# A two-layer encoder step: early convolution taps on ScalarE and GpSimd, later taps summed in PSUM, memory values and some keys as three split products, layer-norm sums added up before TensorE

## The chip, the cores and the metric

The kernel runs on one core of a Trainium2 chip. A core has a matrix engine (TensorE, PE in the profile), a vector engine (VectorE, DVE), a scalar engine (ScalarE, ACT), a general engine (GpSimd, POOL) and a queue that issues transfers (SyncE, SP). Each engine takes its own instructions strictly in order and waits on semaphores for the others. Data lies in SBUF, matrix products go to eight banks of PSUM (128 partitions by 512 words each). The metric is the device time of one launch in microseconds; lower is better. The trace comes from one profiled execution, whose span runs from the first to the last instruction.

## What is computed

One inference step of two layers for two groups that share all weights: 8 running streams of 16 tokens ("sample", 128 tokens) and one new stream of 256 tokens ("prompt"). So all work is on 384 tokens, in three token tiles of 128, with 1024 features.

```python
for i in range(DEPTH):                     # 2 layers
    x = x + 0.5 * rms_norm(swiglu(rms_norm(x)))
    if i % 2 == 0: y = conformer_conv_module(rms_norm(x), ...)
    else:          y = gated_deltanet(rms_norm(x), ...)
    x = x + rms_norm(y)
    x = x + rms_norm(memory_cross_attention(rms_norm(x), mem_k[i], mem_v[i]))
    x = x + 0.5 * rms_norm(swiglu(rms_norm(x)))

# conformer_conv_module
u = h @ w_in + b_in
val, gate = jnp.split(u, 2, axis=-1)
u = val * jax.nn.sigmoid(gate)
hist = jnp.concatenate([conv_buf, u], axis=1)      # 30 earlier rows, then this step's
c = causal_depthwise_conv(hist, dw) + dw_b         # 31 taps per feature
c = jax.nn.silu(layer_norm(c, ln_g, ln_b))
return c @ w_out + b_out, hist[:, -30:]
```

The memory keys and values of the prompt, `p_mem_k` and `p_mem_v`, are 256 memory tokens times one 1024 x 1024 matrix each per layer. They are outputs, and the cross-attention of the prompt reads them back. The sample's come from a cache.

## The kernel before

**Recording and ordering.** The program is first recorded as a list of operations (`Emitter`), and a list scheduler (`Scheduler`) then puts them in order on each engine, by the longest way to the end on costs written in the file. Once ordered, each engine's instructions stand fixed. What waits for nothing else goes where the scheduler sees an engine without other work.

**Weights.** A weight chunk is 128 x 1024 words (512 KB). `get` loads it into one of three raw buffers; ScalarE casts it to the reduced matmul type (the high part, `whi`, line 189) and VectorE subtracts the high part from the raw words (the low part, `wlo`, line 197). Both inputs of that subtraction lie in SBUF. Eight split chunks are held at a time. A product of a chunk and split activations is three matmuls: high times high, high times low, low times high (`gmm`, `dmm`, line 247).

**Memory keys and values.** There are 32 pieces of 128 output features: 8 for keys and 8 for values in each layer. `kv(n)` records the next n of them in plain float32: 16 matmuls of 128 columns each, which show as two records each in the trace. They need only the memory and a raw weight chunk, no splitting, and so can fill TensorE at any time. The table `KV` says how many each place offers: 3 at the start, 3 behind the first feed-forward layer, 20 in the convolution (`conv`), 3 ahead of its output projection (`co`), 1 and 2 behind the next two feed-forward layers.

**The convolution module.** `conv` runs over 8 feature tiles of 128. For each tile two projections (`cg`, `cv`, 24 matmuls of 384 columns each) give gate and value; `glu` makes the sigmoid on ScalarE and two products on VectorE, and copies the prompt's rows into overlapping windows (`h`). `taps` then handles the tiles in pairs. The first 15 taps (`TOLD`) reach only earlier tokens of a sample stream and were already summed for the sample part in `old_taps`, during the feed-forward layer. For the prompt, tap 0 is a `tensor_scalar` of 256 columns and taps 1 to 14 are multiply-adds of 240 down to 227 columns; taps 15 to 30 are 16 multiply-adds of 384 columns (both groups). All of them are on VectorE (lines 204 and 210) and add into `cO` in SBUF, with two tensor inputs in SBUF. Behind each tile one float32 matmul of 384 columns by a matrix of 1/1024 adds its features into the mean, 8 in all.

**Layer norm and output projection.** `ln(t)`, for each token tile: VectorE subtracts the mean, ScalarE squares, 8 float32 matmuls of 128 columns add up the squares, VectorE and GpSimd make the root, one matmul spreads it, VectorE multiplies, ScalarE applies SiLU (8 instructions) and casts, VectorE subtracts for the low part. The output projection (chunks `co`) can begin with the first cast, `hTh`. Nothing else of the program can run on TensorE between the last convolution projection and that point, apart from memory pieces, the layer norm's own matmuls and a bias row (`ones_r`).

Of the kernel before, what the change touches and what calls it, by code (L numbers as in the profile page):

```python
# [58 lines left out]
# constant matrices: causal blocks, block sums, decay masks, block-doubling masks  # L59
# [8 lines left out]
def chunk_names():  # L68
    names = [("mem", 0), ("mem", 1), ("bout",)]
    for l in range(2):  # L70
        for i in range(2):
            for f in range(FF):
                names += [("g", l, i, f), ("u", l, i, f), ("d", l, i, f)]
            names += [(n, l, i, j) for n in ("g4", "u4") for j in range(4)]
        names += [("q4", l, 0, j) for j in range(4)]
        for k in range(KT):
            names += [("wq", l, k), ("wo", l, k), ("wk", l, k // 2, k % 2), ("wv", l, k // 2, k % 2)]
# [16 lines left out]
class Emitter:  # L94
    """Records the program in issue order. Tasks beside the main stream are advanced by running
    clocks of the engines, so that their matmuls fall where their operands are ready."""
# [153 lines left out]
    def quad(self, mms):  # L250
        """Products into four groups of 32 rows, which the tensor engine works on at once."""
# [1538 lines left out]
```

## Time and profile before

| | |
|---|---|
| three runs | 1892.46, 1894.15, 1896.69 us; median 1894.15 us |
| profiled execution | span 1891.9 us |
| median less span | 2.25 us |
| records of TensorE / VectorE / ScalarE / GpSimd | 10863 / 1940 / 1589 / 407 |
| mean granted TensorE clock | 0.998 |
| transfers | 278.83 MB, 147 GB/s over the span |

How to read the views quoted below: a line of the timeline has the start in us from the span's start, the length in us, the engine, the line of the file, the operation, output and inputs (partitions x columns), the number of instructions merged in it, and in brackets how long the engine had stood idle and what released it. A group line has, behind the bar, the busy time in us and the mean ns of one instruction, then the idle time before them. A row of the windows view has the stretch, its length, and the busy time of TensorE, its weight loads, VectorE, ScalarE and GpSimd, the granted clock, the share of the transfer engines and GB/s. Instructions of one engine overlap a little, so the distance between starts is shorter than the mean length. A float32 matmul shows as two records.

### The profile page before, as it was taken

How to read it: one execution, taken by the hardware profiler on the slowest of the kernel's cores; microseconds unless marked ns; L12 is line 12 of the kernel's file. 1: busy time of each engine (PE TensorE's matmuls, PEld its weight loads, DVE VectorE, ACT ScalarE, POOL GpSimd, SP SyncE). 2: the span in 40 equal slices, each digit the busy share in tenths (PEclk: the TensorE clock that was granted, in tenths of full speed). 3: DMA queues.
4: the chain of work that ended last, by engine and by line, in shares of the span. 5: the costliest groups of instructions: out<-in, count | busy, mean ns of one | idle time of the engine just before them, and what ended most of it. 6: DMA issues, size and time to landing. Idle time of an engine off the chain costs nothing.

```text
span 1891.9 us, 27912 instructions
## 1 busy us (share of the span) xinstructions
PE 1870.6 (99%) x10863; PEld 1682.6 (89%) x10863; DVE 1025.5 (54%) x1940; ACT 794.5 (42%) x1589; POOL 168.8 (9%) x407
## 2 busy tenths in 40 slices
PE   8999999999999999999999999999999999999998
PEld 7999999999877899999899999989898767899997
DVE  6564436998653633334633344788886734533333
ACT  4333334312643533233433233787786533433332
POOL 1000002111100100000100000323321101000000
PEclk9999999999999999999999999999999999999999
DMA  8544434556685443434533343433324782444431
GB/s 300 179 136 125 134 112 121 128 147 216 219 312 210 156 129 128 134 123 130 163 122 117 120 134 101 128 97 99 123 90 124 236 311 101 134 134 134 122 123 45
DMA packets 88469, 278.83 MB, mean 147 GB/s; under 512 B 18001, under 2 KB 20561, under 8 KB 88337
## 3 DMA queue, kind: packets, MB, share of 16 engines
q1 hardware_dynamic: 86080, 271.42, 44.7%
q0 software_dynamic: 2256, 5.64, 0.9%
q8 instruction: 85, 1.39, 0.3%
q14 instruction: 48, 0.39, 0.1%
HBM read 265.09 MB, written 11.92 MB: 146 GB/s over the span
## 4 chain that ended last, share of the span: by engine, by line
PE 97%; ACT 1%; DMA 1%; DVE 0%; POOL 0%; issue 0%; SPq 0%; DVEq 0%; POOLq 0%; ACTq 0%
PE ps L247 91%; PE ps L266 3%; PE ps L259 2%; DMA raw<-in_w 0%; POOL stat L197 0%; ACT big L190 0%; DMA x<-in_x 0%; DVE big L210 0%; ACT whi L189 0%; SPq L270 0%; ACT big L189 0%; ACT hTl L190 0%; ACT L190 0%; DVE big L197 0%; DVE wlo L197 0%
## 5 line engine op out<-in xcount | busy, mean ns | idle before, releaser
L197 DVE TENSOR_TENSOR wlo<-raw,whi 128x1024 fp32r<-128x1024 f32 x361 | 438.1, 1221 | 570.7 <-ACT whi L189 542.7
L189 ACT CAST whi<-raw 128x1024 fp32r<-128x1024 f32 x361 | 374.5, 1050 | 640.3 <-PE ps L247 584.6
L247 PE MATMUL ps<-hTh,wlo 128*128 128x384 f32 x1680 | 498.3, 341 | 0.0
L247 PE MATMUL ps<-hTl,whi 128*128 128x384 f32 x1680 | 497.1, 342 | 0.0
L247 PE MATMUL ps<-hTh,whi 128*128 128x384 f32 (+1 forms) x1680 | 496.9, 342 | 0.0
L247 PEld LDWEIGHTS ps<-hTl,whi 128*128 128x128 f32 x1680 | 308.9, 188 | 8.0 <-issue 2.1
L247 PEld LDWEIGHTS ps<-hTh,whi 128*128 128x128 f32 x1680 | 308.8, 188 | 7.9 <-issue 1.2
L247 PE MATMUL ps<-big 128*128 128x128 f32 (+5 forms) x1944 | 308.0, 288 | 7.1 <-DMA big<-in_w 6.7
L247 PEld LDWEIGHTS ps<-hTh,wlo 128*128 128x128 f32 x1680 | 308.7, 188 | 6.5 <-issue 2.3
L247 PEld LDWEIGHTS ps<-big 128*128 128x128 f32 (+1 forms) x1944 | 269.6, 190 | 40.3 <-issue 20.8
L247 PE MATMUL ps<-whi,rbh 128*128 128x512 f32 x672 | 206.0, 396 | 0.4 <-ACT big L189 0.4
L247 PE MATMUL ps<-wlo,rbh 128*128 128x512 f32 x672 | 203.8, 395 | 0.0
L247 PE MATMUL ps<-whi,rbl 128*128 128x512 f32 x672 | 202.5, 393 | 0.0
L210 DVE SCALAR_TENSOR_TENSOR big<-big,cols 128x384 f32<-128x384 f32 (+13 forms) x424 | 189.5, 497 | 2.2 <-ACT big L190 0.3
L247 PEld LDWEIGHTS ps<-whi,rbl 128*128 128x128 f32 x672 | 125.7, 188 | 24.7 <-issue 0.4
L247 PEld LDWEIGHTS ps<-wlo,rbh 128*128 128x128 f32 x672 | 125.3, 188 | 24.6 <-issue 0.4
L247 PEld LDWEIGHTS ps<-whi,rbh 128*128 128x128 f32 x672 | 124.8, 188 | 21.1 <-ACT big L189 0.6
L197 DVE TENSOR_TENSOR big<-big,ps 128x64 f32<-128x64 f32 (+4 forms) x219 | 86.4, 405 | 39.8 <-PE ps L247 39.2
L266 PE MATMUL ps<-ident,big 128*128 128x128 f32 x479 | 89.5, 279 | 5.5 <-DVE big L210 5.4
L247 PE MATMUL ps<-whi,hTh 128*128 128x512 f32 x240 | 87.2, 399 | 0.7 <-ACT hTh L189 0.7
L189 ACT COPY big<-ps 32x32 f32<-32x32 f32 (+5 forms) x155 | 49.6, 324 | 90.2 <-PE ps L247 64.3
L247 PE MATMUL ps<-whi,hTl 128*128 128x512 f32 x240 | 86.3, 398 | 0.0
(82 smaller groups left out, 1350.7 us busy)
## 6 DMA issues: line engine op xcount, KB each, us to landing
raw<-in_w SPq DMA_DIRECT2D x362, 512.0 KB, 3.8
big<-in_w SPq DMA_DIRECT2D x37, 512.0 KB, 5.1
big<-in_ck SPq DMA_DIRECT2D x32, 512.0 KB, 6.5
big<-in_cv SPq DMA_DIRECT2D x32, 512.0 KB, 6.3
big<-in_npre SPq DMA_DIRECT2D x8, 512.0 KB, 7.5
out_pkv<-big POOLq DMA_DIRECT2D x32, 128.0 KB, 5.0
big<-in_npost SPq DMA_DIRECT2D x8, 512.0 KB, 7.3
big<-out_pkv SPq DMA_DIRECT2D x8, 512.0 KB, 5.1
```

The costliest lines, as they stand in the source:

```text
L189: return self._on("A", cost, dep, lambda: sc.copy(out, in_), [in_], w)
L197: return self._on(eng, cost, dep, lambda: e.tensor_tensor(out=out, in0=a, in1=b, op=op), [a, b], [out])
L210: lambda: v.scalar_tensor_tensor(out=out, in0=a, scalar=s, in1=b, op0=op0, op1=op1), [a, s, b], [out])
L247: self._add("P", cost, lambda: t.matmul(out, lhsT, rhs, start=start, stop=stop, **kw), [lhsT, rhs], [out])
L259: t.matmul(out, lhsT, rhs, start=start, stop=stop)
L266: self._add("P", 109.0, lambda: t.transpose(out, in_, ident), [in_, ident], [out])
```

## The change

1. **Values.** All 16 value pieces go into a new function, `kv_split`, in the convolution. Their weights are packed as 16 chunks `v4` of 256 input features by 512 output features. Each is loaded, cast and subtracted like any other weight chunk; the memory is split too (2 chunks, into `rbh`, `rbl`). The product is 192 matmuls of 512 columns.
2. **Keys.** Four of the 16 key pieces go there as well: 4 chunks, 96 matmuls of 256 columns. The other 12 stay in float32, now as 8 matmuls of 256 columns each (`kv`). `KV["conv"]` becomes 4 and means these split keys; the other numbers stay. `SLOTS`, the chunks on chip at the start, goes from 4 to 3.
3. **Early taps.** For the prompt, each of the first 15 taps becomes a product of 256 columns on ScalarE (into one of two halves of `pr`) and, from the second on, an addition of 256 columns on GpSimd into `s`, both inputs in SBUF.
4. **Late taps.** ScalarE puts the sample's sum of old taps and the prompt's tap 15 into a PSUM bank; VectorE adds the rest there (one instruction of 128 columns, 14 of 384), and the last tap goes to `cO` (384). Then VectorE adds `s` to it (256 columns).
5. **Mean.** The eight tiles are added into `total` first (7 additions of 384 columns, five on GpSimd and the last pair's two on VectorE), and one matmul takes the mean.
6. **Squares.** VectorE sums the eight feature tiles of the squares (`rsum`, 1024 inputs, 128 outputs, read with a stride), and one matmul of 128 columns replaces eight.

The rest of the difference is the list of the pieces, the names of the new chunks and removed comments.

```diff
-SLOTS = 4               # chunks of keys and values on chip at the start
+SLOTS = 3
...
-KV = {"start": 3, "f00": 3, "conv": 20, "co": 3, "xo": 0, "f01": 1, "f10": 2, "dn": 6, "f11": 0}
+KV = {"start": 3, "f00": 3, "conv": 4, "co": 3, "xo": 0, "f01": 1, "f10": 2, "dn": 6, "f11": 0}
...
+    def kv_split(self, keys):
+        E = self.E
+        vt = E.vt
+        mh, ml = (a.rearrange("p k c -> p (k c)")[:, 0:2 * D] for a in (self.rbh, self.rbl))
+        for i in range(2):
+            c = slice(i * D, (i + 1) * D)
+            E.get(("mem", i), dest=(mh[:, c], ml[:, c]))
...
+        for l in range(2):
+            for u in range(2):
+                (o, b) = self.bank2()
+                for q in range(4):
+                    j, wh, wl = E.get(("v4", l, u, q))
+                    for k in range(2 * q, 2 * q + 2):
+                        s = slice(512 * (k % 2), 512 * (k % 2) + 512)
+                        for m in range(2):
+                            c = slice(m * P, (m + 1) * P)
+                            E.mm(o[m], mh[:, k, c], wh[:, s], k == 0, False)
+                            E.mm(o[m], mh[:, k, c], wl[:, s], False, False)
+                            E.mm(o[m], ml[:, k, c], wh[:, s], False, k == KT - 1)
...
+        for _ in range(keys):
+            _, l, h, i = self.kvq.pop()
+            j, wh, wl = E.get(("wk", l, h, i))
+            o, b = self.bank()
+            self.gmm(o[:, 0:MEM], wh, wl, 0, MEM, mh, ml)
...
-            for m in range(2):
-                c = slice(m * P, (m + 1) * P)
-                for k in range(KT):
-                    a, b_ = (w[:, k, :], mem[:, k, c]) if kind == "wk" else (mem[:, k, c], w[:, k, :])
-                    E.mm(o[:, c], a, b_, k == 0, k == KT - 1)
+            for k in range(KT):
+                E.mm(o[:, 0:MEM], w[:, k, :], mem[:, k, :], k == 0, k == KT - 1)
...
-                for j in range(CW):
+                for c in cs:
+                    h, o = hist[c][0], accs[c][0]
+                    e1 = E.act(o[:, 0:P], cO[:, c, 0:P], dep=dep)
+                    e1 = E.act(blk(o[:, P:NTOK]), h[:, NB:24, 0:BL], dep=dep, scale=col(C_DW + c * CW + TOLD))
+                e = {c: e1 for c in cs}
+                for j in range(TOLD, CW):
...
-                        if j == 0:
-                            E.ts(cO[:, c, P:], up[:, 0:256], w, ALU.mult, col(C_DWB + c), ALU.add, dep=dep)
-                        elif j < TOLD:
-                            n = CW - 1 - j
-                            o = cO[:, c, P + n:]
-                            e = E.stt(o, up[:, CW - 1:256 + j], w, o, ALU.mult, ALU.add, dep=dep)
+                        if j == TOLD:
+                            e[c] = E.stt(blk(o[:, 0:P]), h[:, 0:NB, 0:BL], w, blk(o[:, 0:P]), ALU.mult, ALU.add, dep=e[c])
                         else:
-                            o = cO[:, c, :].rearrange("p (b i) -> p b i", i=BL)
-                            e = E.stt(o, h[:, :, j - TOLD:j - TOLD + BL], w, o, ALU.mult, ALU.add, dep=dep)
+                            out = blk(o[:, 0:NTOK]) if j < CW - 1 else blk(cO[:, c, :])
+                            e[c] = E.stt(out, h[:, :, j - TOLD:j - TOLD + BL], w, blk(o[:, 0:NTOK]), ALU.mult, ALU.add, dep=e[c])
+                        i = j - TOLD
+                        if i < TOLD:
+                            (s, _), (pr, _) = early[c]
+                            w = col(C_DW + c * CW + i)
+                            if i == 0:
+                                E.act(s, up[:, 0:256], dep=dep, scale=w, bias=col(C_DWB + c))
+                            else:
+                                t = pr[:, 256 * (i % 2):256 * (i % 2) + 256]
+                                ea = E.act(t, up[:, i:i + 256], dep=dep, scale=w)
+                                E.tt(s, s, t, ALU.add, dep=ea, eng="G")
...
-                    E.mm(mean[:, 0:NTOK], self.onesd, cO[:, c, :], c == 0, c == KT - 1)
+                    ep = E.tt(cO[:, c, P:], cO[:, c, P:], early[c][0][0], ALU.add, dep=max(e[c], E.ck["G"]))
...
+                eng = "V" if c0 == KT - 2 else "G"
+                if c0 == 0:
+                    E.tt(total, cO[:, 0, :], cO[:, 1, :], ALU.add, dep=ep, eng=eng)
+                else:
+                    for c in cs:
+                        ep = E.tt(total, total, cO[:, c, :], ALU.add, dep=ep, eng=eng)
...
+            E.mm(mean[0][0][:, 0:NTOK], self.onesd, total, True, True)
...
-        self.kv(KV["conv"])
+        self.kv_split(KV["conv"])
...
-            for k in range(KT):
-                e = E.mm(o[:, 0:P], qv[:, k, :], self.onesd, k == 0, k == KT - 1)
+            e = E.rsum(sq, qv.rearrange("p k c -> p c k"), dep=e)
+            e = E.mm(o[:, 0:P], sq, self.onesd, True, True)
```

The order of instructions on GpSimd (POOL), in the last third of the convolution module. Before, a row is a transfer: `out_pkv` stores memory keys and values, `out_sconv` and `out_pconv` the last rows of the convolution's input.

```order
L236 MEMSET big 128x30
L273 DMA out_sconv<-big 1024x1x30
L273 DMA out_pkv<-big 128x256
L273 DMA out_pconv<-big 128x30
L273 DMA out_sconv<-big 1024x1x30
L273 DMA out_pkv<-big 128x2x128 x2
L273 DMA out_pkv<-big 128x256 x2
```

Now the same stretch holds additions of early products (128x256) and of whole tiles into `total` (128x384), with stores between them:

```order
L273 DMA out_pkv<-big 128x256 x2
L197 TENSOR_TENSOR big<-big 128x256 x5
L197 TENSOR_TENSOR big<-big 128x384
L197 TENSOR_TENSOR big<-big 128x256 x5
L197 TENSOR_TENSOR big<-big 128x384
L197 TENSOR_TENSOR big<-big 128x256
L273 DMA out_pkv<-big 128x256 x2
L197 TENSOR_TENSOR big<-big 128x256
```

From the first addition to the last, GpSimd now has 112 additions of 256 columns, 5 of 384, 13 stores to `out_pkv` and 7 each to `out_sconv` and `out_pconv`.

On VectorE (DVE), the step from the last taps to the layer norm. Before, the last taps (`cols` holds the tap weights) are followed by the subtractions for the bias chunk (`rbl`) and the next weight chunk, and then by the subtraction of the mean, which stands in bank `ps_100`:

```order
L210 SCALAR_TENSOR_TENSOR big<-big,cols 128x384 x81
L197 TENSOR_TENSOR rbl<-raw_87,rbh 128x1024
L197 TENSOR_TENSOR wlo_81<-raw_88,whi_73 128x1024
L197 TENSOR_TENSOR big<-big,ps_100 128x8x128 x2
L197 TENSOR_TENSOR wlo_82<-raw_86,whi_74 128x1024
L197 TENSOR_TENSOR big<-big,ps_100 128x8x128
```

Now additions of the early sums (128x256) and of the last two tiles into `total` (128x384) stand between six weight subtractions and the layer norm:

```order
L210 SCALAR_TENSOR_TENSOR big<-big,cols,ps_98 128x384
L197 TENSOR_TENSOR rbl<-raw_88,rbh 128x1024
L197 TENSOR_TENSOR wlo_79<-raw_86,whi_71 128x1024
L197 TENSOR_TENSOR wlo_80<-raw_87,whi_72 128x1024
L197 TENSOR_TENSOR big<-big 128x256
L197 TENSOR_TENSOR wlo_81<-raw_88,whi_73 128x1024
L197 TENSOR_TENSOR wlo_82<-raw_86,whi_74 128x1024
L197 TENSOR_TENSOR wlo_83<-raw_87,whi_75 128x1024
L197 TENSOR_TENSOR big<-big 128x256
L197 TENSOR_TENSOR big<-big 128x384
```

From its first gate product to the last addition into `total` and on to the norm behind it, VectorE now has 34 such weight subtractions; on TensorE all 384 projection matmuls now stand ahead of the 192 + 96 split products, and these ahead of the mean.

More of the change, by code (lines that the diff above doesn't have):

```diff
@@ L508, in __init__ @@
         self.hready = [0.0] * TT
-        self.kvq = [(k, l, h, i) for l in range(2) for h in range(XH) for k in ("wk", "wv") for i in range(2)]
+        self.kvq = [("wk", l, h, i) for l in range(2) for h in range(XH) for i in range(2)]
         self.kvroom, self.kvs, self.kvn = None, {}, 0
@@ L879, in kv_open, with result @@
         return True
+    def kv_split(self, keys):
[5 more added lines that the diff above has]
+            E.get(("mem", i), dest=(mh[:, c], ml[:, c]))
+        mh, ml = (a.rearrange("p (k m) -> p k m", k=KT) for a in (mh, ml))
+        res, rh = self.alloc(1024)
+        nres = [0]
+        def result(o, n):
+            r = res[:, nres[0] % 2 * 512:nres[0] % 2 * 512 + n]
+            nres[0] += 1
+            E.act(r, o[:, 0:n], dep=0)
+            return r
+        for l in range(2):
[10 more added lines that the diff above has]
+                            E.mm(o[m], ml[:, k, c], wh[:, s], False, k == KT - 1)
+                            E.pump()
+                    E.done(j)
+                for m in range(2):
+                    r = result(o[m], 512)
+                    for n in range(2):
+                        E.store(self.O["pkv"][l, 2 * u + n][:, 512 + m * MEM:512 + (m + 1) * MEM],
+                                r[:, n * MEM:(n + 1) * MEM])
+                self.bfree(b)
+        for _ in range(keys):
[3 more added lines that the diff above has]
+            self.gmm(o[:, 0:MEM], wh, wl, 0, MEM, mh, ml)
+            E.done(j)
+            E.store(self.O["pkv"][l, h][:, i * MEM:(i + 1) * MEM], result(o, MEM))
+            self.bfree(b)
+        self.free(rh)
+        E.vt = vt
     def early(self, what, order):
@@ L998, in taps @@
         def taps():
+            blk = lambda a: a.rearrange("p (b i) -> p b i", i=BL)
+            total, th = yield from self.galloc(NTOK)
             for c0 in range(0, KT, 2):
@@ L1004, in taps @@
                 yield dep
-                for j in range(CW):
+                accs, early = {}, {}
+                for c in cs:
+                    early[c] = (yield from self.galloc(256)), (yield from self.galloc(512))
+                    accs[c] = yield from self.gbank()
+                for c in cs:
+                    h, o = hist[c][0], accs[c][0]
+                    e1 = E.act(o[:, 0:P], cO[:, c, 0:P], dep=dep)
+                    e1 = E.act(blk(o[:, P:NTOK]), h[:, NB:24, 0:BL], dep=dep, scale=col(C_DW + c * CW + TOLD))
@@ L1019, in taps @@
                     yield E.ck["V"] - 1200
                 for c in cs:
-                    self.free(hist[c][1], hist[c][3])
-                    E.mm(mean[:, 0:NTOK], self.onesd, cO[:, c, :], c == 0, c == KT - 1)
-            self.conv_end = e
-        mean, mb = self.bank()
+                    ep = E.tt(cO[:, c, P:], cO[:, c, P:], early[c][0][0], ALU.add, dep=max(e[c], E.ck["G"]))
+                    self.bfree(accs[c][1])
+                    self.free(hist[c][1], hist[c][3], early[c][0][1], early[c][1][1])
@@ new lines, in taps @@
+                eng = "V" if c0 == KT - 2 else "G"
+                if c0 == 0:
+                    E.tt(total, cO[:, 0, :], cO[:, 1, :], ALU.add, dep=ep, eng=eng)
+                else:
+                    for c in cs:
+                        ep = E.tt(total, total, cO[:, c, :], ALU.add, dep=ep, eng=eng)
+            self.conv_end = ep
+            yield ep
+            mean.append((yield from self.gbank()))
+            E.mm(mean[0][0][:, 0:NTOK], self.onesd, total, True, True)
+            self.free(th)
@@ L1026, in conv @@
+        mean = []
         tapper = E.spawn(taps())
@@ L1037, in conv @@
                 prefetch(c + 2)
-        self.kv(KV["conv"])
+        self.kv_split(KV["conv"])
         E.wait(tapper)
+        mean, mb = mean[0]
         E.wait_time(self.conv_end - 3000)
@@ L1061, in ln @@
             o, b = yield from self.gbank()
-            for k in range(KT):
-                e = E.mm(o[:, 0:P], qv[:, k, :], self.onesd, k == 0, k == KT - 1)
+            sq, sqh = yield from self.galloc(P)
+            e = E.rsum(sq, qv.rearrange("p k c -> p c k"), dep=e)
+            yield e
+            e = E.mm(o[:, 0:P], sq, self.onesd, True, True)
+            self.free(sqh)
             v, r = self.st(1), self.st(1)
@@ L1709, in pack @@
             w[i] = g_type(wq[n[1]], n[2] * P)
[L1710 to L1711 removed]
+        elif t == "wk":
+            w[i] = g_type(wk[n[1]], n[2] * MEM + n[3] * P)
         elif t == "wo":
```

19 lines of the change are left out of this document (8 added, 11 removed).

## The prediction

> **What bounds the kernel now.** I read the page first: its busy times and the chain that ended last.
>
> ```profile
> span 1891.9 us, 27912 instructions
> PE 1870.6 (99%) x10863; PEld 1682.6 (89%) x10863; DVE 1025.5 (54%) x1940; ACT 794.5 (42%) x1589; POOL 168.8 (9%) x407
> PE 97%; ACT 1%; DMA 1%; DVE 0%; POOL 0%; issue 0%; SPq 0%; DVEq 0%; POOLq 0%; ACTq 0%
> ```
>
> TensorE sets the end nearly everywhere, so work taken from it counts, as long as no other engine becomes late. The page is a mean over stages, so next come the windows and the timeline of the convolution.
>
> ```profile
> 397.00:454.00 57.00, 57.00 (x493) 55.68 (x492) 56.76 (x114) 6.21 (x16) 11.04 (x17) 1.00 0.55 167
> 454.00:477.00 23.00, 22.08 (x173) 20.57 (x172) 14.84 (x17) 12.84 (x20) 2.93 (x5) 1.00 0.75 264
> ```
>
> ```profile
> 371.20 14.23 DVE L210 SCALAR_TENSOR_TENSOR big<-big,cols 128x229 f32<-128x229 f32 x38
> 396.98 62.49 PE L247 MATMUL ps<-big 128*128 128x128 f32 x528
> 439.89 14.36 DVE L210 SCALAR_TENSOR_TENSOR big<-big,cols 128x384 f32<-128x384 f32 x27
> 457.28 2.35 DVE L197 TENSOR_TENSOR big<-big,ps 128x1024 f32<-128x1024 f32 x2 [0.76 <-PE ps L247]
> 477.04 0.48 PE L247 MATMUL ps<-whi,hTh 128*128 128x512 f32 x1
> ```
>
> From 397 to 454 us **two engines are full at once**: VectorE works off the taps (56.76 of 57 us), and TensorE has nothing left but memory pieces and the mean (records from 396.98 to 459.5). The taps end at 439.89 + 14.36 = 454.2, the layer norm starts at 457.3, and the output projection starts at 477.04. So the pieces are filler for a wait that VectorE causes. Taking away only filler would leave TensorE idle; the change must also bring the start of the output projection forward, and this start is what I predict. Behind it both programs go on alike, except for a few key pieces.
>
> **TensorE's side.**
>
> ```profile
> 491.23 0.39 PE L247 MATMUL ps<-wlo,hTh 128*128 128x512 f32 x1
> 491.46 0.39 PE L247 MATMUL ps<-whi,hTl 128*128 128x512 f32 x1
> 1191.18 0.28 PE L247 MATMUL ps<-hTh,wlo 128*128 128x256 f32 x1
> 1191.30 0.28 PE L247 MATMUL ps<-hTh,whi 128*128 128x256 f32 x1
> L247 PE MATMUL ps<-big 128*128 128x384 f32 x16 | 6.3, 487 | 0.0
> 546.12 1.56 PE L247 MATMUL ps<-big 128*128 128x256 f32 x6
> 561.83 1.13 PE L247 MATMUL ps<-big 128*128 128x256 f32 x4
> ```
>
> Starts lie 0.23 us apart for 512 reduced columns, 0.12 for 256. A float32 record of 128 columns takes 62.49 / 528 = 0.118.
> - 20 pieces x 32 records x 0.118 = 75.7 us go; 192 x 0.23 + 96 x 0.12 = 55.7 come: -20.0.
> - Eight mean matmuls (6.3, the group row) become one (0.8): -5.5.
> - 24 square matmuls, two records each (5.7), become three (0.7): -5.0.
>
> Together -30.5, so TensorE by itself could start the output projection at 477.0 - 30.5 = 446.5. The nine other key pieces change from 3.79 us (32 x 0.118) to 8 matmuls of 256 columns. The last two rows differ by 0.43 for two records; two records of twice 0.118 would be 0.47: a piece is 3.4 to 3.8. Three of them fill the wait anyway; for the rest I take -1, bounds -2 and 0.
>
> **VectorE's side.**
>
> ```profile
> 324.24 0.74 DVE L210 SCALAR_TENSOR_TENSOR big<-ps,cols,big 128x256 f32<-128x256 f32 x2 [0.67 <-ACT big L190]
> 508.57 2.35 DVE L197 TENSOR_TENSOR wlo<-raw,whi 128x1024 fp32r<-128x1024 f32 x2
> ```
>
> A late tap takes 14.36 / 27 = 0.532, an early one 14.23 / 38 = 0.374. Per tile the taps cost 0.4 + 14 x 0.374 + 16 x 0.532 = 14.1 us, for eight tiles 113. Afterwards 112 instructions x 0.532 and 8 of a third of that width (0.26) make 61.7. Gate products stay at 8 x 0.66 = 5.3. New is the splitting of value, key and memory chunks: 34 subtractions up to the norm, each 2.35 - 1.21 = 1.14 (1.21 is a lone one, row 302.74 below), make 38.8. Eight additions of 256 columns (0.40 by the early tap) and two of 384 (0.53) make 4.3. Sum 110.1: if VectorE never waited, it would be through at 324.2 + 110.1 = **434.3 instead of 454.2**. No row shows a tap whose destination is PSUM. [...]
>
> **GpSimd's side** is the new load: 112 additions of 256 columns, 5 of 384, and its stores. It has no such addition before, so I bound it by copies of one input and by a blocked mean.
>
> ```profile
> 1227.12 0.18 POOL L215 COPY big<-big 128x3 f32<-128x3 f32 x1
> 1233.20 0.21 POOL L215 COPY big<-big 128x32 f32<-128x32 f32 x1 [0.97 <-DVE big L210]
> L215 POOL COPY big<-big 128x32 f32<-128x32 f32 x24 | 9.2, 390 | 304.5 <-DVE big L197 251.2 <-PE ps L247 36.5 <-PE ps L259 11.8
> L215 POOL COPY big<-big 128x3 f32<-128x3 f32 x24 | 6.2, 259 | 0.0
> L273 POOL DMA_DIRECT2D out_pkv<-big x26 | 16.8, 647 | 86.6 <-ACT big L189 86.3 <-issue 0.4
> L273 POOL DMA_DIRECT2D out_sconv<-big x8 | 7.0, 881 | 2.3 <-DVE big L210 1.9 <-issue 0.4
> L273 POOL DMA_DIRECT2D out_pconv<-big x8 | 4.4, 555 | 42.7 <-DVE big L210 42.7
> ```
>
> Alone, 29 more columns cost 0.03 us, 1 ns a column. Low end, as with one input: 0.18 + 0.26 = 0.44. Taken, two inputs at twice that: **0.70**. High end, by the slope of the means (131 ns for 29 columns): 1.3. The taken value is nearest to the undisturbed rows. So 112 x 0.70 = 78.4, 5 x 0.97 = 4.9, and 13, 7 and 7 stores (0.65, 0.88, 0.56) 18.5: 101.8 us.
>
> [...]
>
> Now the collision. The small statistics on GpSimd show it:
>
> ```profile
> 291.45 0.57 POOL L197 TENSOR_TENSOR stat<-stat,negh 128x1 f32<-128x1 f32 x1
> 302.74 1.21 DVE L197 TENSOR_TENSOR wlo<-raw,whi 128x1024 fp32r<-128x1024 f32 x1
> 302.78 1.60 POOL L197 TENSOR_TENSOR stat<-stat,negh 128x1 f32<-128x1 f32 x1
> 309.40 0.68 DVE L197 TENSOR_TENSOR hTl<-ps,hTh 128x512 fp32r<-128x512 f32 x1
> 309.61 0.56 POOL L197 TENSOR_TENSOR stat<-stat,negh 128x1 f32<-128x1 f32 x1
> ```
>
> The same instruction takes 0.57 alone, 0.56 beside a VectorE operation with one input in PSUM, and 1.60 beside a weight subtraction, whose two inputs lie in SBUF: **1.03 lost, nearly the whole subtraction**. Late taps in PSUM don't hurt GpSimd, then, but each of the 34 subtractions can. GpSimd's stores leave it 82% on additions: 34 x 0.82 x 1.03 = 28.7, and 3.2 for the eight additions on VectorE. It starts when the first tile's windows and products are there, about 326. Sum: 326 + 101.8 + 28.7 + 3.2 = **460**, later than VectorE's 434 and TensorE's 446.
>
> [...]
>
> ScalarE gets 120 products:
>
> ```profile
> L190 ACT ACTIVATE big<-ps,stat 128x256 f32<-128x256 f32 x48 | 21.7, 478 | 41.9 <-PE ps L259 31.0 <-issue 5.6 <-DVE stat L204 5.1
> ```
>
> At up to 0.478 (an end that overlaps the next included) they are 57 us, with some 40 casts and copies of about 1 us at most still below the 134 us that GpSimd has; this cost is hidden unless ScalarE's order stalls (second rival).
>
> **The norm.**
>
> ```profile
> 467.01 1.05 ACT L189 CAST whi<-raw 128x1024 fp32r<-128x1024 f32 x1 [3.42 <-DMA raw<-in_w]
> 469.85 1.05 ACT L189 CAST whi<-raw 128x1024 fp32r<-128x1024 f32 x1 [1.79 <-DMA raw<-in_w]
> 472.21 3.57 ACT L190 ACTIVATE big<-big,cols 128x128 f32<-128x128 f32 x9
> L233 DVE TENSOR_REDUCE big<-big 128x32 f32<-128x128 f32 x24 | 8.8, 375 | 0.1
> L228 DVE TENSOR_REDUCE stat<-ps 128x2 f32<-128x512 f32 x16 | 11.0, 691 | 24.7 <-PE ps L259 21.0 <-PE ps L247 3.4
> ```
>
> After GpSimd's last addition come the early sum (0.40), the total (0.53), the mean matmul (0.8) and hand-offs (0.6): the norm starts at 462.3. Before, it lasted 477.04 - 457.28 = 19.8, with two stalls of ScalarE for raw weights (3.42 and 1.79) ahead of SiLU. Those chunks now have longer to land. Its path becomes three mean subtractions (3.4), three reductions, statistics (0.5), two weight subtractions (2.3), a multiplication (1.2), eight SiLU (3.57 / 9 = 0.40 each, 3.2), the cast (1.0), hand-offs (0.4). A reduction of 1024 inputs is between 1.2 (twice 691 ns less a fixed part) and 1.75 (by the strided groups of 128 inputs, 375 ns with overlap); between near ends I take 1.45, 4.3 for three. Sum 16.3: the output projection starts at **478.6, 1.6 later than before**.
>
> **The sum.** 1891.9 + 1.6 - 1 = 1892.5 of span. The median lies 2.25 above the profiled span: 1894.7, no change within the 0.2% (4 us) that a measurement of this kernel can tell.
>
> **Rivals.**
> - *The collision costs little* (chance 0.25): subtractions fall on stores or on times in which GpSimd waits for a tile, or an addition takes 0.5 us. Then GpSimd is through at 428, VectorE at 434 binds, and the output projection starts at 434.3 + 2.3 + 16.3 = 453, still behind TensorE's 446.5: -24 - 1, some 1869. For it speaks that TensorE, GpSimd and VectorE all have their sums below 447 without the 28.7; against it, that GpSimd never gets ahead of VectorE by more than a pair of tiles.
> - *ScalarE stands in line behind GpSimd* (0.20): a product needs one of two halves of `pr`, which GpSimd frees. Casts, gates and result copies stand behind it in ScalarE's strict order, and GpSimd waits for a product (0.41) and two hand-offs, 0.8 us, each time that ScalarE has been held by a 1 us cast. At some 24 casts that fall among the products this is 19 us more on GpSimd's 460: 1914, slower. It decides from the point at which GpSimd has used up both halves, since two additions last only 1.4 us.
> [...]
>
> **Chances and range.** The forecast has 0.50. An addition of 0.60 to 0.80 alone moves it by 11 us either way: own range 1884 to 1906 (faster 0.16, same 0.18, slower 0.16). With the rivals: faster 0.16 + 0.25, same 0.18 + 0.05, slower 0.16 + 0.20. The range goes from below the first rival, 1866, to above the second, 1916; the high end of the addition (+67 us) is left out.
>
> **What would show it.** In the profile after: GpSimd full up to about 460, additions of 0.7 alone and 1.7 beside a weight subtraction; TensorE idle for 25 to 35 us ahead of the mean matmul, released through VectorE by GpSimd; taps in PSUM at 0.53; about 16 us from norm to output projection. Wrong if VectorE's last tap is what the mean waits for, if ScalarE is seen waiting for GpSimd often, or if the value matmuls wait for weights.

## The result, and the profile after

The changed kernel takes 1939.9 us (median of 4 runs, 1938.0 to 1941.8) against 1893.8 before: 1.0244 times as long, 95% interval 1.0228 to 1.0259. The forecast was 1894.7, its range ended at 1916. The page of the changed kernel, its busy times and the chain that ended last:

```profile
span 1937.9 us, 26992 instructions
PE 1864.9 (96%) x10263; PEld 1653.4 (85%) x10263; DVE 1027.9 (53%) x1855; ACT 878.0 (45%) x1745; POOL 278.9 (14%) x524
PE 90%; DVE 5%; issue 2%; ACT 1%; DMA 1%; POOL 1%; SPq 0%; DVEq 0%; POOLq 0%; ACTq 0%
```

TensorE's busy time fell by only 5.7 us although 30 us of work were taken away, the span grew by 46, and 5% of the chain now runs over VectorE (0% before). The mean granted clock fell from 0.998 to 0.985; 1.3% of 1865 us is 24 us, which would be what the busy time does not show as saved. The windows view, by stage (columns: stretch, length, busy us of TensorE, its weight loads, VectorE, ScalarE, GpSimd, granted clock, transfer share, GB/s), shows where TensorE stands still or runs slowly:

```profile
0.00:333.00 333.00, 309.35 (x1591) 282.25 (x1592) 162.35 (x271) 117.58 (x174) 14.04 (x38) 0.99 0.46 149
333.00:407.00 74.00, 69.86 (x388) 69.05 (x387) 56.58 (x83) 51.57 (x100) 46.94 (x63) 0.95 0.49 134
407.00:495.00 88.00, 63.10 (x295) 52.07 (x293) 81.67 (x114) 56.41 (x102) 78.39 (x93) 0.87 0.57 165
495.00:515.00 20.00, 15.50 (x66) 12.46 (x66) 16.02 (x15) 14.07 (x27) 5.46 (x7) 0.82 0.76 194
1480.00:1535.00 55.00, 49.80 (x255) 38.93 (x254) 30.85 (x63) 34.99 (x102) 11.10 (x23) 0.95 0.44 146
```

In the convolution (333 to 515) TensorE is 33 us short of full (148.5 busy of 182), and the clock falls with it. But 333 us passed before the convolution began, 20 more than before, and there is a hole at 1480 to 1535 that was not there. The loss has three places. Four marks split it: the first matmul of the convolution's projections, the start of the layer norm (its first subtraction of the mean), the first matmul of the output projection, and the end.

| profiled execution, us | first projection at | to the norm | norm to output projection | from there to the end | span |
|---|---|---|---|---|---|
| before | 312.6 | 144.7 | 19.8 | 1414.8 | 1891.9 |
| after | 333.2 | 161.7 | 20.2 | 1422.9 | 1937.9 |
| difference | +20.6 | +17.0 | +0.4 | +8.0 | +46.0 |

**Ahead of the convolution**, the waits of TensorE (engine, line, releaser: us in all, times, longest) and one tile of the first feed-forward layer on VectorE and TensorE:

```profile
PE ps L247 <- DVE big L197: 15.8, 12, 1.3
```

```profile
78.15 1.23 DVE L197 TENSOR_TENSOR wlo<-raw,whi 128x1024 fp32r<-128x1024 f32 x1 [9.66 <-PE ps L247]
79.29 0.55 DVE L197 TENSOR_TENSOR big<-big,ps 128x384 f32<-128x384 f32 x1
79.89 0.44 PE L247 MATMUL ps<-hTh,whi 128*128 128x384 f32 x1 [1.31 <-DVE big L197]
```

A feed-forward tile ends with a product on VectorE that frees a bank, and the next tile needs the bank. The same place in the kernel before:

```profile
79.08 2.58 DVE L197 TENSOR_TENSOR wlo<-raw,whi 128x1024 fp32r<-128x1024 f32 x2 [6.08 <-ACT whi L189]
80.18 1.56 PE L247 MATMUL ps<-wlo,rbh 128*128 128x512 f32 x6
81.57 1.53 PE L247 MATMUL ps<-whi,rbl 128*128 128x512 f32 x6
81.58 0.55 DVE L197 TENSOR_TENSOR big<-big,ps 128x384 f32<-128x384 f32 x1
```

There TensorE had down-projection matmuls (512 columns) of an earlier tile to do while VectorE made the product. After the change the planner puts those ahead of the tile's last matmuls, and TensorE waits 1.31 us in each of 12 tiles, 15.8 of the 20.6 us. The rest shows as busy time (309.4 us against 304.5 before) and was not taken apart. The change edits nothing in this loop.

**In the convolution**, the groups on GpSimd and VectorE between the first projection and the norm, and a moment that shows how they meet:

```profile
L197 POOL TENSOR_TENSOR big<-big 128x256 f32<-128x256 f32 x112 | 100.5, 931 | 9.9 <-ACT big L190 9.1
L197 DVE TENSOR_TENSOR wlo<-raw,whi 128x1024 fp32r<-128x1024 f32 x36 | 59.6, 1669 | 17.4 <-PE ps L247 10.5 <-ACT whi L189 3.8 <-ACT big L190 3.0
```

```profile
466.44 9.56 POOL L197 TENSOR_TENSOR big<-big 128x256 f32<-128x256 f32 x11
468.24 7.18 DVE L197 TENSOR_TENSOR wlo<-raw,whi 128x1024 fp32r<-128x1024 f32 x1
474.30 1.70 POOL L197 TENSOR_TENSOR big<-big 128x256 f32<-128x256 f32 x1
475.47 0.58 PE L247 MATMUL ps<-rbh,wlo 128*128 128x256 f32 x1 [4.97 <-DVE wlo L197]
480.50 3.80 POOL L197 TENSOR_TENSOR big<-big 128x256 f32<-128x256 f32 x1 [1.41 <-ACT big L190]
485.67 2.62 DVE L197 TENSOR_TENSOR wlo<-raw,whi 128x1024 fp32r<-128x1024 f32 x1 [1.97 <-ACT whi L189]
493.20 1.62 PE L247 MATMUL ps<-big 128*128 128x384 f32 x2 [7.70 <-DVE big L197]
```

Eleven additions stand back to back on GpSimd, and one subtraction of 1.2 us on VectorE lasts 7.18. While it stands, eight additions begin and end on GpSimd, at about 0.7 us each; only the next one, the last of the eleven (474.30), is held up in its turn and takes 1.70. TensorE waits 4.97 us for the subtraction's result. At 480.5 it is the other way round: one addition lasts 3.80 while three subtractions run. GpSimd's last addition is through at 487.2, but the mean matmul starts at 493.2, since VectorE still has three weight subtractions ahead of its last additions, and these wait in part for ScalarE's casts of raw weights.

The longest wait of TensorE in the convolution is another one:

```profile
416.76 1.13 DVE L210 SCALAR_TENSOR_TENSOR big<-big,cols,ps 128x384 f32<-128x384 f32 x2
417.42 0.79 PE L247 MATMUL ps<-whi,rbh 128*128 128x512 f32 x1 [9.59 <-DVE big L210]
446.62 0.50 PE L247 MATMUL ps<-whi,rbh 128*128 128x512 f32 x1 [2.33 <-DVE big L210]
```

The late taps now hold a PSUM bank for each of the two tiles in work. The last tap of a tile (`big<-big,cols,ps`) reads its bank for the last time. The first of the two in row 416.76 ends at 417.37, and 0.05 us later a value product begins; at 446.6 it is the same. So TensorE stands for a bank that the taps hold, 11.9 of its 33.5 us of waits here; nine_early waits for the same operation of VectorE too (11.7 us in two waits, the longest 9.0). That it is the bank is read from the order of the two and from the code; no run gave the taps other banks. The prediction has no such term.

**Behind the deltanet** TensorE waits for VectorE at the last token tile's row; before the change its longest wait for VectorE at this place was 0.63:

```profile
1531.47 1.12 PE L266 MATMUL ps<-ident,big 128*128 128x128 f32 x4 [4.26 <-DVE big L210]
```

The clock is at half (0.50) from 1529.8 to 1536.6 us, behind and during this wait. What else makes up the 8.0 us was not followed.

### The profile page after: what moved, and what is told of

It reads as the page before. It is cut to its first block, busy times and chain, and to the rows that moved or that the text cites. A ratio compares the mean times of both kernels' runs of the same rounds, so it can differ in the third digit from the quotient of the medians.

```text
span 1937.9 us, 26992 instructions
## 1 busy us (share of the span) xinstructions
PE 1864.9 (96%) x10263; PEld 1653.4 (85%) x10263; DVE 1027.9 (53%) x1855; ACT 878.0 (45%) x1745; POOL 278.9 (14%) x524
## 3 DMA queue, kind: packets, MB, share of 16 engines
q8 instruction: 80, 1.31, 0.3%
## 4 chain that ended last, share of the span: by engine, by line
PE 90%; DVE 5%; issue 2%; ACT 1%; DMA 1%; POOL 1%; SPq 0%; DVEq 0%; POOLq 0%; ACTq 0%
PE ps L247 85%; PE ps L266 3%; PE ps L259 2%; DVE wlo L197 2%; DVE ps L210 2%; DMA raw<-in_w 1%; DVE big L197 1%; ACT big L190 1%; POOL stat L197 1%; DVE big L210 0%; ACT whi L189 0%; DMA x<-in_x 0%; DVE big L233 0%; DVE hTl L197 0%; ACT hTl L190 0%
## 5 line engine op out<-in xcount | busy, mean ns | idle before, releaser
L197 DVE TENSOR_TENSOR wlo<-raw,whi 128x1024 fp32r<-128x1024 f32 x381 | 477.6, 1264 | 599.7 <-ACT whi L189 468.2
L189 ACT CAST whi<-raw 128x1024 fp32r<-128x1024 f32 x381 | 396.2, 1052 | 691.6 <-PE ps L247 639.4
L247 PE MATMUL ps<-hTh,whi 128*128 128x384 f32 x1680 | 515.6, 344 | 20.2 <-DVE big L197 15.8
L247 PEld LDWEIGHTS ps<-hTh,whi 128*128 128x128 f32 x1680 | 311.0, 189 | 33.3 <-DVE big L197 20.0
L247 PE MATMUL ps<-whi,rbh 128*128 128x512 f32 x736 | 229.0, 399 | 12.0 <-DVE big L210 11.9
L247 PE MATMUL ps<-big 128*128 128x128 f32 (+5 forms) x1056 | 220.3, 320 | 14.1 <-DVE big L197 7.7
L247 PE MATMUL ps<-wlo,rbh 128*128 128x512 f32 x736 | 225.7, 396 | 0.0
L247 PE MATMUL ps<-whi,rbl 128*128 128x512 f32 x736 | 224.9, 396 | 0.0
L247 PEld LDWEIGHTS ps<-big 128*128 128x128 f32 (+1 forms) x1056 | 173.5, 190 | 47.8 <-issue 23.3
L197 POOL TENSOR_TENSOR big<-big 128x256 f32<-128x256 f32 x117 | 105.1, 935 | 10.3 <-ACT big L190 9.1
L204 POOL TENSOR_SCALAR stat<-stat 128x1 f32<-128x1 f32 (+2 forms) x48 | 16.9, 352 | 553.8 <-ACT hTl L190 539.3
```

The source lines that it names most:

```text
L189: return self._on("A", cost, dep, lambda: sc.copy(out, in_), [in_], w)
L197: return self._on(eng, cost, dep, lambda: e.tensor_tensor(out=out, in0=a, in1=b, op=op), [a, b], [out])
L204: return self._on(eng, cost, dep, lambda: e.tensor_scalar(out=out, in0=a, scalar1=s1, scalar2=s2, op0=op0, **kw), [a, s1, s2 if s2 is not ...
L247: self._add("P", cost, lambda: t.matmul(out, lhsT, rhs, start=start, stop=stop, **kw), [lhsT, rhs], [out])
```

## The experiments

Eleven kernels ran. The marks of their profiled executions (us; the norm starts with the first subtraction of the mean):

| run | first projection at | to the norm | norm to output projection | from there to the end | span |
|---|---|---|---|---|---|
| slots4 | 311.2 | 160.3 | 23.0 | 1426.1 | 1920.5 |
| taps_only | 312.0 | 174.6 | 17.4 | 1425.7 | 1929.7 |
| kv_only | 310.6 | 180.6 | 18.9 | 1417.0 | 1927.0 |
| small_adds | 334.1 | 149.1 | 23.8 | 1422.9 | 1929.9 |
| small_subs | 334.5 | 141.4 | 21.9 | 1420.6 | 1918.4 |
| slots4_subs_last | 311.8 | 152.9 | 20.5 | 1422.4 | 1907.5 |
| before_slots3 | 311.4 | 151.4 | 16.9 | 1423.7 | 1903.4 |
| nine_early | 313.1 | 155.0 | 20.5 | 1423.2 | 1911.8 |
| ten_early_mix | 311.0 | 155.4 | 22.9 | 1428.2 | 1917.4 |
| before_plan_a | 309.1 | 145.0 | 19.3 | 1422.8 | 1896.1 |
| before_plan_b | 312.8 | 145.3 | 17.7 | 1420.1 | 1895.8 |

**slots4: the changed kernel with four slots.**

```diff
-SLOTS = 3
+SLOTS = 4
```

> The changed kernel with SLOTS = 4 instead of 3; nothing else. With it the order on VectorE in the loop of the first feed-forward layer is again, for most tiles, product, its low part, three weight subtractions, as before the change. Theory A (about 20 of the 46 us arise ahead of the convolution, because with three slots the scheduler settles into another order of that loop, in which TensorE waits 1.3 us in 12 tiles for VectorE's product): the first matmul of the convolution's projections comes at 313 to 316 us instead of 333.2, and the whole time falls by 17 to 20 us, to 1920 to 1923. Rival B (the loss ahead of the convolution comes from the transfers and pieces at the start): the fall is 2 to 3 us at most, to 1937. In both the convolution from its first projection to the first matmul of the output projection stays at about 180 us.

Measured: 1926.2 us, 1.0171 (1.0156 to 1.0186). The first projection comes at 311.2, 22 us earlier, and ahead of it no wait for VectorE's product is left; these are all waits of TensorE there:

```profile
PE ps L247 <- DMA big<-in_w: 6.4, 2, 4.9
PE ps L266 <- DVE big L210: 1.1, 1, 1.1
```

Theory A holds for the place: 20 of the 46 us come from an order ahead of the convolution. Its times are missed by 2 us (313 to 316 for the first projection) and 3 us (1920 to 1923 in all). The whole time fell less (17 in the profiled execution, 14 by the medians), since 3 us were lost again behind the output projection and 1 in the convolution.

**taps_only and kv_only: one half of the change each.** The first puts the new taps, mean and squares into the kernel before, with `self.kv(KV["conv"])` as it was and 20 float32 pieces. The second takes the changed kernel with four slots and puts the old taps, mean and squares back.

> The kernel before with the change's parts 3 to 6 alone (early taps on ScalarE and GpSimd, late taps in PSUM, summed mean, summed squares); all memory pieces stay in float32, 20 of them in the convolution, so VectorE has 10 weight subtractions there instead of 34. Theory A (the collision of weight subtractions with GpSimd's additions makes the loss in the convolution): with so few of them GpSimd and VectorE are through before TensorE, whose float32 pieces bind; from the first projection to the output projection 150 to 157 us against 164.4 before and 181.9 after the change, whole time 1882 to 1890. Rival B (GpSimd's additions by themselves are too slow): the stretch stays at 172 or more and the time lies above 1900.

> The changed kernel's parts 1 and 2 alone, with SLOTS = 4: values and four keys as split products, the other keys in float32 matmuls of 256 columns; taps, mean and squares as before. Theory A (VectorE is what the convolution waits for, and 24 more weight subtractions of 1.14 us go onto it): the last tap comes 20 to 27 us later than before, and the whole time is 1908 to 1921. Rival B (TensorE binds, and 20 us of its work are gone): the time is 1872 to 1880.

Measured: taps_only 1927.6 us, 1.0183 (1.0168 to 1.0198); kv_only 1929.4, 1.0192 (1.0175 to 1.0209). Each half alone is 34 to 36 us slower than before. In kv_only the last tap ends at 487.1 instead of 454.2: theory A's cause, though by 33 us instead of 20 to 27, and its band for the whole time (1908 to 1921) is missed too. GpSimd has no such additions there, and the subtractions keep their length (mean 1218 ns), so this loss comes without any collision: up to the norm VectorE is busy for 159.3 us instead of 133.3, and it waits 11 us longer, for casts above all. taps_only missed theory A widely. Its numbers are those of rival B, but B's reason, additions that are too slow by themselves, does not show: their mean is 802 ns, and the last one is through at 459.4, 27 us ahead of the norm. On VectorE between the first projection and the norm:

```profile
L197 DVE TENSOR_TENSOR wlo<-raw,whi 128x1024 fp32r<-128x1024 f32 x18 | 39.1, 2179 | 17.6 <-ACT whi L189 17.6
422.40 11.52 DVE L197 TENSOR_TENSOR wlo<-raw,whi 128x1024 fp32r<-128x1024 f32 x2 [1.14 <-ACT whi L189]
447.69 1.88 DVE L197 TENSOR_TENSOR big<-big 128x256 f32<-128x256 f32 x1 [13.77 <-POOL big L197]
```

With fewer subtractions the collision got worse for each: 18 with a mean of 2179 ns, two of them 11.5 us together. VectorE stands 13.8 us before an early sum that GpSimd has not finished, while the last pair's taps stand behind it in line, and then 6.8 us more until ScalarE has filled their bank. At the end the collision is no longer what counts: VectorE is through at 475.1, but the norm waits 11.4 us for the mean from TensorE, which is held by float32 pieces whose result copies on ScalarE wait up to 7.4 us for stores to `out_pkv`. How the 35 us divide among these was not tested.

**small_adds and small_subs: the order held, one side made short.** On every engine the instructions stand as in the changed kernel; only the width of one kind shrinks.

```diff
-                                E.tt(s, s, t, ALU.add, dep=ea, eng="G")
+                                E._on("G", 130 + 2.3 * 256, ea, lambda s=s, t=t: E.nc.gpsimd.tensor_tensor(
+                                    out=s[:, 0:16], in0=s[:, 0:16], in1=t[:, 0:16], op=ALU.add), [s, t], [s])
...
-        self.tt(lo, raw, hi.bitcast(F32), ALU.subtract)
+        if name[0] in ("cg", "cv", "v4", "wk", "mem", "co", "bout"):
+            self._on("V", 65 + 1.05 * self._n(lo), None, lambda: self.nc.vector.tensor_tensor(
+                out=lo[:, 0:16], in0=raw[:, 0:16], in1=hi.bitcast(F32)[:, 0:16], op=ALU.subtract), ...)
```

> The changed kernel, its order on every engine held word for word, but the 112 additions of early products on GpSimd work on 16 columns instead of 256 (so the early taps' sums are left out of the result for the most part). Theory A (GpSimd's additions, by their length and by holding back weight subtractions, set the end of the convolution): from the first projection to the start of the layer norm 128 to 138 us instead of 161.7; no subtraction on VectorE of more than 2 us; whole time 1905 to 1914. Rival B (ScalarE's products or the subtractions themselves set it): that stretch shrinks by less than 10 us, whole time 1928 or more.

> The changed kernel with its order on every engine held, but the weight subtractions of the convolution (projections, memory, values, keys, bias, output projection) work on 16 columns instead of 1024 (most of these low parts are left out of the result). Theory A (VectorE and GpSimd shut each other out while both inputs of a VectorE operation lie in SBUF): GpSimd's 112 additions fall from a mean of 931 ns to 740 to 800, the length of an undisturbed one, and its stretch from the first to the last addition from 136 to 112 to 122 us, since it now binds; the layer norm starts 20 to 30 us earlier than in the changed kernel. Rival B (an addition of 256 columns is 0.9 us on GpSimd whatever VectorE does): the mean stays above 870 and the last addition comes less than 8 us earlier.

Measured (one run each): small_adds 1932.0 us, small_subs 1920.5. The two groups in question, VectorE's subtractions with short additions, then GpSimd's additions with short subtractions:

```profile
L197 DVE TENSOR_TENSOR wlo<-raw,whi 128x1024 fp32r<-128x1024 f32 x36 | 44.1, 1237 | 17.8 <-PE ps L247 10.6 <-ACT whi L189 6.7 <-ACT big L190 0.5
```

```profile
L197 POOL TENSOR_TENSOR big<-big 128x256 f32<-128x256 f32 x112 | 80.9, 756 | 8.3 <-ACT big L190 7.6
```

Each gives the other nearly its undisturbed length back (1.21 us for a lone subtraction, 0.74 for a lone addition): 36 subtractions fall from a mean of 1669 to 1237 ns (15.5 us), 112 additions from 931 to 756 (19.6 us). So the collision is real and hits both sides. small_subs is as theory A had it: the first to the last addition takes 117.1 us instead of 136.1, and the norm starts 20.3 us sooner, counted from the first projection. That gain is not the collision's alone, since short subtractions also relieve VectorE itself of 41 us. small_adds is between the two in the convolution, where the stretch to the norm shrinks by 12.6 us, to 149.1, not to 128 to 138; its whole time is rival B's. With short additions VectorE sets the end: from its last tap (467.9) to the norm (483.2) it still works off six subtractions, three of which wait for casts of raw weights. GpSimd, too, is through only at 473.6, since it stands 44.8 us for ScalarE's products.

**slots4_subs_last: the output projection's subtractions behind the additions.**

```diff
-SLOTS = 3
+SLOTS = 4
...
-        self.tt(lo, raw, hi.bitcast(F32), ALU.subtract)
+        late = [self.total] if name[0] in ("co", "bout") else []
+        self._on("V", 65 + 1.05 * self._n(lo), None, lambda: self.nc.vector.tensor_tensor(
+            out=lo, in0=raw, in1=hi.bitcast(F32), op=ALU.subtract), [raw, hi.bitcast(F32)] + late, [lo])
```

> The changed kernel with SLOTS = 4, and the planner is told that the low parts of the bias chunk and of the output projection's first chunks wait for the finished total. So on VectorE the additions of the early sums and into the total stand directly behind the last taps, and the weight subtractions behind them. Theory A (behind GpSimd's last addition VectorE still works off weight subtractions ahead of the additions, which is part of the loss in the convolution): from the last tap to the layer norm 3 to 6 us instead of 16.6 in the run with four slots alone; output projection 6 to 10 us earlier unless the low parts are now late; whole time 1910 to 1917. Rival B (GpSimd's last addition sets the start of the norm, and the subtractions only fill the wait for it): the norm starts less than 3 us earlier, time 1920 to 1925.

Measured: 1913.6 us, 1.0106 (1.0091 to 1.0121), the lowest of the kernels with the change (nine_early below is level with it). From the last tap to the norm 10.8 us instead of 16.6, not 3 to 6. What is left is the wait for GpSimd:

```profile
452.73 1.13 DVE L210 SCALAR_TENSOR_TENSOR big<-big,cols,ps 128x384 f32<-128x384 f32 x2
460.22 3.13 DVE L197 TENSOR_TENSOR big<-big 128x256 f32<-128x256 f32 x4 [6.36 <-POOL big L197]
464.62 1.22 DVE L197 TENSOR_TENSOR big<-big,ps 128x1024 f32<-128x1024 f32 x1
```

The norm starts 6.8 us earlier and the output projection 9.3. Theory A holds for the norm, with GpSimd next in line.

**before_slots3: no change of work at all.**

```diff
-SLOTS = 4
+SLOTS = 3
```

> The kernel before with SLOTS = 3 instead of 4, nothing else. The order in the loop of the first feed-forward layer is of the same kind as before; the order of the token tiles behind the gated delta network's output projection is the one of the changed kernel. Theory A (it is the orders, not the number of slots or the work, that cost time at both places): no waits of TensorE in the first feed-forward loop, the convolution as before within 4 us, but 4 to 8 us lost from the deltanet's end to the attention behind it: 1896 to 1904. Rival B (three slots themselves cost the loop its speed): 17 us or more lost ahead of the convolution, 1910 or more.

Measured: 1906.8 us, 1.0074 (1.0057 to 1.0091). No wait in the feed-forward loop (first projection at 311.4): three slots in themselves don't cost the 20 us. But 8.9 us are lost behind the output projection, and behind the deltanet stands the very wait of the changed kernel, where the work is the same as before:

```profile
1498.02 1.12 PE L266 MATMUL ps<-ident,big 128*128 128x128 f32 x4 [4.26 <-DVE big L210]
```

So the third loss, too, is one of order. The time is 2 to 3 us above theory A's band: the convolution lost 3.8 us as well.

**nine_early and ten_early_mix: GpSimd relieved.** Early taps from `TG` on go to VectorE, in PSUM; the second also has five split keys and `NRUSH = 4`.

```diff
+                        if TG <= i < TOLD:
+                            e[c] = E.stt(o[:, P:NTOK], up[:, i:i + 256], col(C_DW + c * CW + i), o[:, P:NTOK], ...)
-                        if i < TOLD:
+                        elif i < TG:
```

> As the run with four slots and the subtractions last, but only taps 0 to 8 of the prompt go over ScalarE and GpSimd; taps 9 to 14 are added on VectorE into the PSUM bank (48 instructions of 256 columns, at some 0.37 us 18 us in all), so GpSimd has 48 additions less (36 us by their undisturbed 0.74, some 45 with collisions). Theory A (GpSimd's last addition sets the norm's start, and its back-to-back additions hold VectorE's subtractions back): GpSimd is through at some 430 instead of 462, subtractions above 2 us vanish, and VectorE binds with its last tap at 456 to 462; norm at 459 to 466 instead of 464.6; whole time within 1900 to 1909. Rival B (VectorE has no room at all): its last tap comes 18 us later than 453.9, the norm at 475, whole time 1916 to 1920.

> As the run before, with taps 0 to 9 over GpSimd, five split keys in the convolution instead of four and one number of the planner changed (NRUSH 4 instead of 3), which puts operations in another order. Theory A (with VectorE and GpSimd balanced the convolution comes down to the level of the kernel before, and what is left is the order behind the gated delta network): norm at 455 to 462, whole time 1893 to 1903. Rival B (the collision eats what the balance gives): norm at 464 or later, 1907 or more. A time below 1892 would beat both kernels; I don't expect it.

Measured: 1915.0 us, 1.0108 (1.0093 to 1.0123), and 1923.3, 1.0162 (1.0145 to 1.0179). Both miss theory A; the second is in rival B's band (norm at 466.4), the first in neither. In nine_early no subtraction takes over 2 us any more, as theory A had it. But with 48 additions fewer GpSimd is still through only at 463.7, not at 430: in nine_early it stands 22.1 us for products of ScalarE and 12.5 for VectorE. VectorE's last tap moves from 453.9 to 464.5, by 10.6 us, and the norm to 468.1. So VectorE had room for some 7 of the 18 us. The loads can be shifted between the two, but together they are too much for the stretch.

**before_plan_a and before_plan_b: the kernel before in another order.** Planner numbers alone (HALF, CHB, HOP; NRUSH, TAIL).

> The kernel before with three numbers of the planner changed (HALF 700 instead of 1400, CHB 5000 instead of 4000, HOP 150 instead of 100): the same operations, another order. Theory A (an order is worth up to some 10 us in this kernel, either way, with the same work): the time differs from the kernel before by more than 0.2%, 1885 to 1905, and the difference sits in waits of TensorE at a few places, not in busy time. Rival B (the order matters only where the change added work): within 0.2% of the kernel before.

> The kernel before with two other numbers of the planner changed (NRUSH 4 instead of 3, TAIL 4 instead of 3): the same operations, another order. Theory A and rival B as for the run before this one: 1885 to 1905 and more than 0.2% away, or within 0.2%.

Measured: 1897.1 us, 1.0020 (1.0011 to 1.0029), and 1897.9, 1.0025 (1.0015 to 1.0036). Both are at the edge of theory A: an order costs 4 us net here, not 10, and in both the convolution is as before (164.3 and 163.0 from first projection to output projection); the loss is behind it. None of the eleven is faster than the kernel before.

## Why the prediction was wrong

By its own steps; the forecast span was 1892.5, the measured one 1937.9, 45.4 more.

- **The step that failed most: the change was costed only where it was made.** "Behind it both programs go on alike", and GpSimd's start at 326 was taken from the trace of before. The program is put in order by a planner over its whole length, and both ends came out in another order: +20.6 us ahead (shown by slots4, where the waits vanish with one number) and +8.0 behind instead of -1 (shown by before_slots3, where the same wait appears without any change of work). That is 29.6 of the 45.4.
- **GpSimd's stretch came out right, in part by luck.** 134 us forecast from the first to the last addition, 136.1 measured (351.1 to 487.2); an addition alone 0.74 us against 0.70. The loss by collision (28.7 forecast for subtractions) is 19.6 by small_subs, and GpSimd also waited 9.1 us for products, which the forecast put at nothing: two errors that nearly cancel. Its start, 18.0 us behind the first projection instead of 13.4, costs 4.6 more.
- **The hand-over was mis-sized**: 2.3 us from GpSimd's last addition to the norm, measured 7.6 (487.2 to 494.9). The order shown in the section on the change has weight subtractions ahead of the last additions; the forecast counted them in VectorE's sum, but not their place. slots4_subs_last gains 6.8 us at the norm by moving them. "GpSimd full up to about 460" was to be what the mean waits for; in the changed kernel the chain that ended last passes over VectorE's taps and subtractions and over raw weights between 404 and 493 us, and over no addition of GpSimd.
- **The norm was mis-sized**: 16.3 forecast, 20.2 measured. The three reductions take 1.87 us each instead of 1.45, above the 1.75 that was taken as their upper bound: 1.3 us. The first cast, `hTh`, is through at 512.8, but TensorE still works on memory pieces that stand ahead of the output projection in its order, 2.3 us more (the rows below). The errors of GpSimd's start, its stretch, the hand-over and the norm (4.6, 2.1, 5.3 and 3.9) are together the 16 us by which the convolution missed: +17.4 instead of +1.6.

```profile
512.20 3.18 PE L247 MATMUL ps<-big 128*128 128x256 f32 x14
515.03 0.58 PE L247 MATMUL ps<-whi,hTh 128*128 128x512 f32 x1
```

- **VectorE was taken to be through well ahead of GpSimd, and it is the second bound.** The forecast gave it 110.1 us from its first gate product to its last addition, if it never waited; it took 143.6, of which it was busy for 130.8. The 36 subtractions of the stretch lost 15.5 us of that to the collision (small_adds). The price is not spread: a single one lost 6 us with TensorE waiting for it, and in taps_only 18 of them lost 17 us. In the changed kernel's trace the engine with more such instructions in line kept the other one out over several of them: 7.18 us for a subtraction while eight additions passed, 3.80 for an addition beside three subtractions.
- **TensorE's prices were right** at full clock (0.23 and 0.12 us a matmul), but the 30 us that it saved are idle time: its waits between the first projection and the output projection sum to 33.5 us (0.9 before), and it ran slowly behind the long ones; the mean matmul took 1.62 us at half clock instead of 0.8. The forecast had 25 to 35 us of idle time, but ahead of the mean matmul; 7.7 of the 33.5 lie there, and 11.9 are the waits for the taps' banks.
- The rivals: the first (collision costs little) is refuted by small_subs. The second had the sign, but another cause: ScalarE did wait for GpSimd (13.4 us in 19 places), yet GpSimd stood only 9.1 us for products. The late taps came out as taken: the trace of before shows none in PSUM, the forecast gave them the 0.532 us of a tap in SBUF, and one in PSUM takes 0.53 (2.71 for five) on VectorE. What it costs besides is the bank.

What stays open: why the planner settles into the worse order of the feed-forward loop with three slots and the new pieces was not tried further than by slots4; and the 4.7 us by which the first gate product comes later appears in before_slots3 too (4.8), so it is one of order as well, but its place was not followed. How much of the convolution's loss is the collision and how much VectorE's load and order is not divided either: small_subs and small_adds change both at once.

## What to carry to other kernels

In a program that a planner puts in order as a whole, compare the order also where the change edits nothing, loops above all: 1.3 us in each of 12 tiles of a loop, 15.8 us, cost nearly as much as the convolution lost in all (17.4). Before work is moved from VectorE to GpSimd, list what VectorE still does with two inputs in SBUF in that stretch, since their meetings cost 15.5 us on VectorE and 19.6 on GpSimd here, and the highest prices fell on the one that met the other with several such instructions in line (7.18 us for a subtraction of 1.2). A sum that is moved into PSUM also holds a bank that TensorE may want (11.9 us of waits here). And work taken from an engine that only fills a wait gains nothing until what it waits for is sooner.

## What the runs showed of the hardware

In the changed kernel TensorE ran at half its clock behind each wait of 2.33 us or more, the program's start aside. Behind the wait of 4.97 us at 475.5 us (clock 0.55 from 475.4 to 478.8) the matmuls of 256 columns start 0.21 us apart, and some 3 us later 0.12 again:

```profile
476.28 0.41 PE L247 MATMUL ps<-rbh,wlo 128*128 128x256 f32 x1
476.49 0.41 PE L247 MATMUL ps<-rbh,whi 128*128 128x256 f32 x1
479.04 0.28 PE L247 MATMUL ps<-rbh,wlo 128*128 128x256 f32 x1
479.16 0.28 PE L247 MATMUL ps<-rbh,whi 128*128 128x256 f32 x1
```

The granted clock of the convolution's second half is 0.87 by the windows above, where it was 1.00 before. The shortest of the waits that half clock follows are those of 3.07 us at 1650.2 (0.50 from there to 1656.0) and of 2.33 us at 446.6, where half clock begins 1.2 us behind the wait (the row below, clock 0.50). The 12 waits of 1.31 us in the feed-forward loop left the clock at 1.00. No wait between 1.32 and 2.33 us occurs in this trace.

```profile
447.80:451.10 3.30, 3.30 (x10) 2.53 (x9) 1.53 (x3) 3.30 (x9) 2.50 (x4) 0.50 0.54 160
```

So these waits were paid twice: the one at 475.5 us with 4.97 us of idle time, and with 3 us in which the matmuls behind it took nearly twice as long each (0.21 us instead of 0.12).

A reduction over 1024 strided inputs took VectorE 1.9 us (5.60 for three), where its subtractions of 1024 columns took 1.2 (3.48 for three from PSUM, 1.22 for one in SBUF).
